# Pacing, an earlier root, interleaved transposes and sums from copies at the joint between two projections

## The chip, the cores and the metric

The kernel runs on one core of a Trainium2 chip. The metric is device time in microseconds (us): what one execution takes on the core. The engines are named PE (TensorE), DVE (VectorE), ACT (ScalarE), POOL (GpSimd) and SP (SyncE, which issues the transfers). Each works through its own instructions in the order in which the program gave them.

## The reference

Two transformer blocks on a sequence of 1024 tokens with 1024 channels, in float32. The part around the change is the end of the second block:

```python
merged = g_a * (o_a @ w_branch_a[l]) + g_b * (o_b @ w_branch_b[l])
x = x + merged @ w_out[l]
h2 = rms_norm(x, norm2[l])
x = x + jnp.square(jax.nn.relu(h2 @ w_up[l])) @ w_down[l]
return rms_norm(x, final_norm)
```

`rms_norm` multiplies a row by the reciprocal root of its mean square and by a gain per channel.

## The kernel before

**Precision.** Each float32 operand is split into a high part (a rounding copy on ACT, `e.hi`) and a low part (the difference, `e.lo`, on POOL or DVE). A product is three matmuls: high by high, low by high, high by low.

**Seven products.** The projection `merged @ w_out`, the up projection and the down projection are each cut in 2 x 2 quadrants and computed with seven products in place of eight (Strassen's scheme in Winograd's form). Products 2 to 7 need sums or differences of quadrants as operands: `cb`, `wr` (of weights, line 838), `ms` (of activations, `m_sums`), `s1` to `s4` (of the up projection's activations, `prep1`). The order of products is ORDER = (1, 6, 7, 4, 2, 5, 3); the text counts products of the output projection by their place in it, from 1 to 7. Each has four tiles of 12 matmuls of 512 columns (four `q` by three matmuls, for each of four row tiles).

**How order is made.** The program is written out by a Python generator that keeps a planned clock `e.t`, moved on by `e.pe` with each matmul. `e.at(dt, fn, tag)` puts a piece of work of another engine on a heap; it is written out when the planned clock reaches its time, or earlier by `e.need(tag)`. Nothing on the chip looks at this clock: it sets only the order on each engine. Instructions wait for the data by semaphores.

**Feeds.** A `Feed` (`FO` for the output projection, `F` for the up projection) holds a list of steps: a weight difference on DVE (`comb`) or a split (`split`: ACT, and with the next step the low part on POOL, or on DVE in 5 of 14 for `FO`). `ahead(n)` and `s.need(mark, n)` set a goal; up to it `tick` writes one step out each `gap` ns of planned time; a step that is not out when its operand is used is forced. `look` says how many steps further the loads are issued. `FO` has 72 steps: products 1 to 7 end at steps 8, 28, 36, 48, 56, 64, 72. In `F`, for the first three column groups (N0 = 3), steps 1 to 3 split operand 1; then for each q come the split of operand 2 and four differences (4 to 18); then three splits each for operands 4, 5, 6, 7 and 3.

**Stages around the change.** `merge` makes `mT` in eight rounds j and starts `FO`. `out2` runs the seven products; `out2_gather` adds each bank to the residual `x` (DVE, line 1554), takes a square sum (ACT, `sumsq`, tile `junk`) and, once both column halves are there, `f3` has POOL form the reciprocal root (`ry`, lines 117 and 118) and DVE scale the row (`xs`, line 1567). There are six row buffers, so rows 6 and 7 (`held`) are scaled when `prep0` has let go of the first four. `prep0` transposes the scaled rows of the first half into two banks in turn (`tp`); ACT copies each twice (`hh`, `hr`, lines 1677 and 1678) and DVE forms `hl` (line 1679). `prep1` does the second half: per k it transposes two banks, `p21` and `p22`, and DVE forms three sums straight from them with the first half's `r11` (line 1700), and the low part. `up_first` runs the up projection's products for three column groups: 3 tiles each for operands 1, 2, 4, 5, 6, 7, 3. At the end of the stage a helper joins generators: `prep0` is written between the matmuls of `out2`, its rest behind them; `prep1` between those of `up_first`, one step per four groups of three matmuls.

The helper records every matmul at line 99, every transpose at 104, and splits at 109 (high) and 112 (low), so rows are told apart by tile names.

Of the kernel before, what the change touches and what calls it, by code (L numbers as in the profile page):

```python
# [11 lines left out]
F32 = mybir.dt.float32  # L12
# [286 lines left out]
def block_kernel(ctx: ExitStack, tc: tile.TileContext, a: dict):  # L299
# [655 lines left out]
            e.mm(ps[:, c2], wl[:, c], h[:, c2], False, k == KT - 1)  # L955
            yield 327.0

    def interleave(main, side, start, every):

        side, n = side(), 0  # L960
        for _ in main:
            t = start()
            if side is not None and t is not None and e.t >= t:
                n += 1
                if n % every == 0:
                    try:
                        next(side)
                    except StopIteration:
                        side = None
        if side is not None:  # L970
            run(side)

    qsc = [[2.0 ** (2 * p + j - 2) for j in range(2)] for p in range(4)]
# [513 lines left out]
    def merge():  # L1487
        g_load(0)
        for j in range(8):
            if j < 7:  # L1490
                g_load(j + 1)
            parts = W.get(f"ab{j}", 1)
            if j == 5:
                for q in range(4):
                    FO.raw[q, "a", 1] = mT[q, 1]
                FO.load(0, 8)
            if j > 5:
                FO.ahead(8 * (j - 5))
            for half in range(2):
                ps2 = []  # L1500
                for b in range(2):
                    ps = e.mmt()
                    wh, wl = parts[b]
                    for k in range(4):
                        c = slice(k * 128, k * 128 + 128)
                        e.need(("o", 4 * b + k, half))
                        h, l = oT[4 * b + k, half]
                        e.mm(ps, wh[:, c], h, k == 0, False)
                        e.mm(ps, wh[:, c], l, False, False)
                        e.mm(ps, wl[:, c], h, False, k == 3)  # L1510
                        yield 650.0
                    g = gt.pop((b, j, half))
                    e.at(50, lambda ps=ps, g=g: V.scalar_tensor_tensor(out=g, in0=g, scalar=1.0, in1=ps,
                                                                       op0=ALU.add, op1=ALU.mult))
                    ps2.append(g)
                ga, gb = ps2
                e.at(800, lambda ga=ga, gb=gb: V.tensor_tensor(out=ga, in0=ga, in1=gb, op=ALU.add))
                mT[j, half] = ga
            if j >= 4:
                e.at(1800, lambda q=j - 4: m_sums(q), ("ms", j - 4))  # L1520
            W.pop(f"ab{j}")
# [10 lines left out]
    def out2():  # L1532
        for n, i in enumerate(ORDER):
            if n < 4:
                for t in range(4):
                    x2_load(i, t)
            if n >= 4:
                F.load(0, n - 3)
                F.ahead(6 * (n - 4))
            e.wide = i not in (5, 3)  # L1540
            yield from row_prod(FO, i, range(4), 16, out2_gather)

    def x2_load(i, t):
        t, ch = where(i, t)
# [6 lines left out]
    def out2_gather(i, t, ps):  # L1551
        t, ch = where(i, t)
        xt = x2[t, ch]
        V.scalar_tensor_tensor(out=xt, in0=ps, scalar=0.5, in1=xt, op0=ALU.mult, op1=ALU.add)
        if i not in (4, 2, 5, 3):
            return
        if ch == 0:
            ss2[t] = e.stat(name="ss2")
        ss = ss2[t]
        e.at(750, lambda: sumsq(xt, ss[:, ch:ch + 1]))  # L1560
        if ch == 1:
            def f3():
                POOL.tensor_tensor(out=ss[:, 2:3], in0=ss[:, 0:1], in1=ss[:, 1:2], op=ALU.add)
                r = e.rstd(ss[:, 2:3])
                xs = e.row("xs")
                for j in range(2):
                    V.tensor_scalar(out=xs[:, 512 * j:512 * j + 512], in0=x2[t, j], scalar1=r, scalar2=None, op0=ALU.mult)
                xs2[t] = xs

                def f4():  # L1570
                    for j in range(2):
                        SY.dma_start(out=x2_d[t * 128:(t + 1) * 128, 512 * j:512 * j + 512], in_=x2.pop((t, j)))
                e.at(2500, f4)
            if t < 6 or rows_free:
                e.at(1650, f3, ("xs2", t))
            else:
                held.append((f3, ("xs2", t)))
            xs2_t[t] = e.t + 4450


    F = Feed()
# [106 lines left out]
    def prep1():  # L1688
        for t in range(4, 8):
            e.need(("xs2", t))  # L1690
        for k in range(4):
            if k > 1:
                e.need(("s2", k - 2))
            two = e.ssp.tile([128, 1024], F32, name="S", tag="S") if k % 2 else None
            p21, p22 = (tr4(1, k + 4 * j, None if two is None else two[:, 512 * j:512 * j + 512]) for j in range(2))
            g1, g2 = gains[:, 2, k:k + 1], gains[:, 2, k + 4:k + 5]
            r11, r12 = HR.pop(("11", k)), HR.pop(("12", k))
            x21, s1, s3, s2 = (e.u(name="hr") for _ in range(4))
            h, l = HA["22", k] = e.u(F32R, "hh"), e.u(F32R, "hl")
            stt = lambda out, ps, g, y, op: V.scalar_tensor_tensor(out=out, in0=ps, scalar=g, in1=y, op0=ALU.mult, op1=op)  # L1700
            e.at(50, lambda p22=p22, h=h, g2=g2: ACT.activation(h, p22, AF.Copy, scale=g2))
            e.at(50, lambda p21=p21, x21=x21, g1=g1: ACT.activation(x21, p21, AF.Copy, scale=g1))
            e.at(800, lambda p21=p21, s3=s3, g1=g1, r11=r11: stt(s3, p21, g1, r11, SUB))
            e.at(1500, lambda p22=p22, s1=s1, g2=g2, x21=x21: stt(s1, p22, g2, x21, ADD))
            e.at(2200, lambda p22=p22, l=l, g2=g2, h=h: stt(l, p22, g2, h.bitcast(F32), SUB), ("A", "22", k))
            e.at(2900, lambda p22=p22, s2=s2, g2=g2, s3=s3: stt(s2, p22, g2, s3, ADD), ("s2", k))
            asplit("s1", k, s1, 2400, POOL)
            asplit("s3", k, s3, 4500, POOL)
            asplit("s2", k, s2, 5500, V)
            e.at(12000 + 1000 * k, lambda r12=r12, s2=s2: V.tensor_tensor(out=r12, in0=r12, in1=s2, op=SUB))  # L1710
            asplit("s4", k, r12, 14000 + 1000 * k, POOL)
            yield 872.0
        for t in range(4, 8):
            xs2.pop(t)

    def prod(ps, q, i, first=True, ahead=11):
        wh, wl = F.take((q, i), ahead)
        for k in range(4):
            e.need(("A", ANAME[i], k))
            h, l = HA[ANAME[i], k]  # L1720
            c = slice(k * 128, k * 128 + 128)
# [44 lines left out]
    def up_first():  # L1766
# [8 lines left out]
        for q in qs:  # L1775
            X[q] = ps = e.mmt()
            yield from prod(ps, q, 1, True, 6)
            e.at(50, lambda q=q, ps=ps: keep(1, q, ps), ("keep", q))
        for q in qs:
            ps = X.pop(q)  # L1780
            e.need(("keep", q))
# [74 lines left out]
                e.at(50, lambda q=q: keep(3, q, X[q]), ("u3", q))  # L1856
                e.at(750, lambda q=q: total(q, Vb[q], 3, "22"), ("c22", q))

    interleave(out2(), prep0, lambda: xs2_t.get(3), 2)
    interleave(up_first(), prep1, lambda: xs2_t[7], 4)  # L1860
    e.wide = True
    F.look = 11
    run(up_pairs(N0))
# [116 lines left out]
```

## Time and profile before

| | us |
|---|---|
| median of 3 runs | 1864.5 |
| lowest, highest | 1864.38, 1864.9 |
| the profiled execution | 1863.2 |
| its span, first to last instruction | 1861.5 |

The mean granted clock of TensorE over the span is 0.989 of full speed. All rows are of the one profiled execution; times in them count from its first instruction. "x12" is a count; a name such as `mm<-hh,fh` is the tile written, then the tiles read. A bracket behind a row is the idle time of the engine just before it, with what ended it.

### The profile page before, as it was taken

What the parts mean: (1) busy time and instruction counts of PE and PEld (TensorE: products, weight loads), DVE (VectorE), ACT (ScalarE), POOL (GpSimd) and SP (SyncE); (2) the same over time, 40 slices, a digit from 0 to 9 for tenths busy, and PEclk for the clock granted to TensorE, in tenths of its full rate; (3) what the DMA queues carried; (4) which work ended last, traced back from release to release, by engine and by line L of the source; (5) the groups of instructions that cost most, each with busy time, mean ns of one, the idle gap of its engine ahead of it and who ended that gap; (6) DMA issues with size and microseconds to landing.
All of it is one profiled execution on the core that took longest, in us unless ns stands there. A gap on an engine that the chain in (4) does not pass through costs nothing.

```text
span 1861.5 us, 25745 instructions
## 1 busy us (share of the span) xinstructions
PE 1802.8 (97%) x8957; PEld 1513.3 (81%) x8957; DVE 1132.7 (61%) x2081; ACT 962.3 (52%) x1979; POOL 733.7 (39%) x704
## 2 busy tenths in 40 slices
PE   7999999999999999999999999779999998999998
PEld 6888878898898898889888887558888876888886
DVE  6578783645454556655675485576443347766785
ACT  6455453447656667554565214465555554352444
POOL 4123242512212212212111425556544445775873
PEclk9999999999999999999999999889999999999999
DMA  7101132314222212120213923203635368444522
GB/s 203 34 24 35 35 114 69 125 35 92 80 46 85 76 39 60 57 71 26 63 38 107 300 68 119 75 11 128 218 127 183 126 240 303 158 151 138 170 85 91
DMA packets 189187, 195.69 MB, mean 105 GB/s; under 512 B 16944, under 2 KB 124160, under 8 KB 189056
## 3 DMA queue, kind: packets, MB, share of 16 engines
q1 hardware_dynamic: 189056, 194.04, 33.1%
q8 instruction: 70, 1.15, 0.3%
q14 instruction: 61, 0.50, 0.1%
HBM read 141.52 MB, written 54.04 MB: 105 GB/s over the span
## 4 chain that ended last, share of the span: by engine, by line
PE 86%; DVE 6%; issue 3%; ACT 3%; POOL 2%; DMA 1%; POOLq 0%; SPq 0%; ACTq 0%; DVEq 0%
PE mm L99 37%; PE mmmm L99 14%; PE mmT L99 9%; PE mmO L99 7%; PE mmo L99 5%; PE tp L104 4%; PE S L99 4%; PE O L99 4%; POOL fl L112 1%; DVE wr L838 1%; DVE s L1055 1%; ACT junk L404 1%; POOL ry L118 0%; DMA ha<-hid_d 0%; DVE sb L665 0%
## 5 line engine op out<-in xcount | busy, mean ns | idle before, releaser
L112 POOL TENSOR_TENSOR wl<-wr,wh 128x512 fp32r<-128x512 f32 x148 | 198.5, 1347 | 561.7 <-ACT wh L109 320.5
L99 PE MATMUL mm<-hh,wh 128*128 128x512 f32 (+1 forms) x792 | 313.8, 396 | 0.0
L99 PE MATMUL mm<-hl,wh 128*128 128x512 f32 (+1 forms) x792 | 310.1, 392 | 1.1 <-DVE hl L940 1.1
L99 PE MATMUL mm<-hh,wl 128*128 128x512 f32 (+1 forms) x792 | 309.5, 391 | 0.0
L112 POOL TENSOR_TENSOR fl<-wr,fh 128x512 fp32r<-128x512 f32 x161 | 228.7, 1434 | 146.4 <-ACT fh L109 122.1
L109 ACT CAST fh<-wr 128x512 fp32r<-128x512 f32 x216 | 130.4, 617 | 222.0 <-DVE wr L838 170.1
L656 ACT ACTIVATE sb<-sb,nm 128x128 f32<-128x128 f32 (+2 forms) x192 | 125.7, 655 | 149.4 <-DVE nm L650 99.0
L99 PEld LDWEIGHTS mm<-hh,wl 128*128 128x128 f32 x792 | 149.8, 189 | 32.5
L99 PEld LDWEIGHTS mm<-hl,wh 128*128 128x128 f32 x792 | 150.2, 190 | 26.1 <-DVE hl L940 1.6
L99 PEld LDWEIGHTS mm<-hh,wh 128*128 128x128 f32 x792 | 150.2, 190 | 25.3
L112 DVE TENSOR_TENSOR ptl<-tp,pth 128x512 fp32r<-128x512 f32 (+2 forms) x176 | 113.5, 646 | 79.8 <-ACT pth L109 75.8
L112 POOL TENSOR_TENSOR fl<-ha,fh 128x512 fp32r<-128x512 f32 x80 | 122.0, 1542 | 48.9 <-ACT fh L109 35.8
L109 ACT CAST pth<-tp 128x512 fp32r<-128x512 f32 (+2 forms) x176 | 96.4, 548 | 74.0 <-PE tp L104 69.8
L665 DVE TENSOR_SCALAR sb<-sb,rc 128x128 f32<-128x128 f32 (+2 forms) x192 | 97.6, 508 | 6.7
L104 PE MATMUL tp<-ident,sb 128*128 128x128 f32 x648 | 99.7, 272 | 1.3 <-DVE ptl L112 1.0
L109 ACT CAST wh<-wr 128x512 fp32r<-128x512 f32 x148 | 89.9, 617 | 20.7 <-DMA wr<-in_w_branch_a 16.1
L104 PEld LDWEIGHTS tp<-ident,sb 128*128 128x128 f32 x648 | 80.5, 140 | 22.9 <-DVE ptl L112 1.8
L838 DVE TENSOR_TENSOR wr<-wr 128x512 f32<-128x512 f32 x108 | 95.0, 880 | 1.6
L99 PE MATMUL O<-pth,v 128*128 128x256 f32 (+3 forms) x264 | 93.2, 361 | 0.0
L99 PE MATMUL mmmm<-fh 128*128 128x512 f32 x212 | 83.4, 393 | 6.7 <-ACT fh L109 6.7
L99 PE MATMUL mmmm<-fl,fh 128*128 128x512 f32 x212 | 83.8, 395 | 2.4 <-POOL fl L112 1.8
L99 PE MATMUL mmmm<-fh,fl 128*128 128x512 f32 x212 | 83.0, 391 | 0.0
(319 smaller groups left out, 4586.0 us busy)
## 6 DMA issues: line engine op xcount, KB each, us to landing
wr<-in_w_in SPq DMA_DIRECT2D x116, 256.0 KB, 3.4
ha<-hid_d SPq DMA_DIRECT2D x112, 256.0 KB, 3.7
wr<-in_w_up SPq DMA_DIRECT2D x64, 256.0 KB, 3.8
hid_d<-hc SPq DMA_DIRECT2D x64, 256.0 KB, 2.7
wr<-in_w_down SPq DMA_DIRECT2D x64, 256.0 KB, 4.2
hid_d<-pk SPq DMA_DIRECT2D x45, 256.0 KB, 3.8
wr<-in_w_out SPq DMA_DIRECT2D x32, 256.0 KB, 5.0
x_d<-x SPq DMA_DIRECT2D x32, 256.0 KB, 2.1
```

The costliest lines, as they stand in the source:

```text
L99: self.nc.tensor.matmul(out=out, lhsT=lhsT, rhs=rhs, start=start, stop=stop, skip_group_check=skip)
L104: self.nc.tensor.transpose(out, in_, ident)
L109: self.nc.scalar.copy(out, in_)
L112: (eng or self.nc.vector).tensor_tensor(out=out, in0=in0, in1=hi.bitcast(F32), op=ALU.subtract)
L404: ACT.activation(j[:, 0:n], src, AF.Square, accum_out=acc)
L656: ACT.activation(d[:, 0:w], d[:, 0:w], AF.Exp, bias=nm, scale=-1.0, accum_out=g.sm[:, j:j + 1])
L665: V.tensor_scalar(out=d[:, 0:w], in0=d[:, 0:w], scalar1=g.rc[:, j:j + 1], scalar2=None, op0=ALU.mult)
L838: eng.tensor_tensor(out=self.raw[dst], in0=self.raw[x], in1=self.raw[y], op=op)
L1055: V.tensor_tensor(out=nxt[:, a0:1040], in0=cur[:, a0:1040], in1=cur[:, a0 - n:1040 - n], op=ALU.add)
```

## The change

1. `FO` writes a step each 800 ns of planned time (1500 before); its goals are 8, then 20 steps in the last rounds of `merge` (8, 16 before), and in `out2` 20 ahead in the first two products and 28 after (16 before). `F` gets a goal of 8 in product 7 (before: 0, 6 and 12 in products 5 to 7).
2. In `out2_gather` the root is written 1650 ns after the gather as before, and the scaling in a function of its own at 3000 ns.
3. What is left of `prep0` after `out2` is returned by `interleave(..., True)` and written inside `up_first`, one step per two groups; `prep1` follows it in the same generator, one step per four groups.
4. In `prep1` both banks are copied out (`x21` on ACT as before, `x22` on DVE); the low part and the sums are formed from the copies, and the sums are queued behind the fourth transposes (`sums_a`). Transposes no longer wait for `s2`.

```diff
@@
     FO = Feed()
-    FO.look = 8
+    FO.look, FO.s.gap = 8, 800.0
@@
             if j > 5:
-                FO.ahead(8 * (j - 5))
+                FO.ahead(8 if j == 6 else 20)
@@
             if n >= 4:
                 F.load(0, n - 3)
-                F.ahead(6 * (n - 4))
+            if n == 6:
+                F.ahead(8)
             e.wide = i not in (5, 3)
-            yield from row_prod(FO, i, range(4), 16, out2_gather)
+            yield from row_prod(FO, i, range(4), 20 if n < 2 else 28, out2_gather)
@@
             def f3():
-                POOL.tensor_tensor(out=ss[:, 2:3], in0=ss[:, 0:1], in1=ss[:, 1:2], op=ALU.add)
-                r = e.rstd(ss[:, 2:3])
                 xs = e.row("xs")
                 for j in range(2):
-                    V.tensor_scalar(out=xs[:, 512 * j:512 * j + 512], in0=x2[t, j], scalar1=r, scalar2=None, op0=ALU.mult)
+                    V.tensor_scalar(out=xs[:, 512 * j:512 * j + 512], in0=x2[t, j], scalar1=rs[0], scalar2=None, op0=ALU.mult)
                 xs2[t] = xs
...
+            def f2():
+                POOL.tensor_tensor(out=ss[:, 2:3], in0=ss[:, 0:1], in1=ss[:, 1:2], op=ALU.add)
+                rs.append(e.rstd(ss[:, 2:3]))
+            e.at(1650, f2, ("rs2", t))
+
+            def f23():
+                e.need(("rs2", t))
+                f3()
             if t < 6 or rows_free:
-                e.at(1650, f3, ("xs2", t))
+                e.at(3000, f23, ("xs2", t))
             else:
-                held.append((f3, ("xs2", t)))
-            xs2_t[t] = e.t + 4450
+                held.append((f23, ("xs2", t)))
+            xs2_t[t] = e.t + 4900
@@ prep1
         for k in range(4):
-            if k > 1:
-                e.need(("s2", k - 2))
...
-            x21, s1, s3, s2 = (e.u(name="hr") for _ in range(4))
+            x21, x22 = raw[k] = e.u(name="hr"), e.u(name="hr")
...
-            e.at(800, lambda p21=p21, s3=s3, g1=g1, r11=r11: stt(s3, p21, g1, r11, SUB))
-            e.at(1500, lambda p22=p22, s1=s1, g2=g2, x21=x21: stt(s1, p22, g2, x21, ADD))
-            e.at(2200, lambda p22=p22, l=l, g2=g2, h=h: stt(l, p22, g2, h.bitcast(F32), SUB), ("A", "22", k))
-            e.at(2900, lambda p22=p22, s2=s2, g2=g2, s3=s3: stt(s2, p22, g2, s3, ADD), ("s2", k))
-            asplit("s1", k, s1, 2400, POOL)
-            asplit("s3", k, s3, 4500, POOL)
-            asplit("s2", k, s2, 5500, V)
-            e.at(12000 + 1000 * k, lambda r12=r12, s2=s2: V.tensor_tensor(out=r12, in0=r12, in1=s2, op=SUB))
-            asplit("s4", k, r12, 14000 + 1000 * k, POOL)
+            e.at(50, lambda p22=p22, x22=x22, g2=g2: V.tensor_scalar(out=x22, in0=p22, scalar1=g2, scalar2=None, op0=ALU.mult))
+            e.at(800, lambda x22=x22, l=l, h=h: e.lo(l, x22, h), ("A", "22", k))
+            if k == 3:
+                for n in range(4):
+                    e.at(1600 + 1500 * n, lambda n=n: sums_a(n, *raw.pop(n)), ("sa", n))
             yield 872.0
@@
+    def sums_a(k, x21, x22):
+        r11, r12 = HR.pop(("11", k)), HR.pop(("12", k))
+        s3, s2 = e.u(name="hr"), e.u(name="hr")
+        V.tensor_tensor(out=s3, in0=x21, in1=r11, op=SUB)
+        V.tensor_tensor(out=x21, in0=x21, in1=x22, op=ADD)
+        V.tensor_tensor(out=s2, in0=x22, in1=s3, op=ADD)
+        asplit("s1", k, x21, 700, POOL)
+        asplit("s3", k, s3, 4500, POOL)
+        asplit("s2", k, s2, 5500, V)
+        e.at(9000 + 1000 * k, lambda: V.tensor_tensor(out=r12, in0=r12, in1=s2, op=SUB))
+        asplit("s4", k, r12, 11000 + 1000 * k, POOL)
@@
-    interleave(out2(), prep0, lambda: xs2_t.get(3), 2)
-    interleave(up_first(), prep1, lambda: xs2_t[7], 4)
+    first = interleave(out2(), prep0, lambda: xs2_t.get(3), 2, True)
+
+    def preps():
+        if first is not None:
+            yield from first
+        for _ in range(200):
+            if e.t >= xs2_t[7]:
+                break
+            yield
+        for _ in prep1():
+            yield
+            yield
+    while first is not None and ("11", 3) not in HA:
+        next(first)
+    interleave(up_first(), preps, None, 2)
```

`prod` gets one more line, which writes a pending `sums_a` out before an operand that needs it.

## Rows read from the trace of the kernel before

**Rows 1.** Page, part 1: busy time of the engines.
```profile
PE 1802.8 (97%) x8957; PEld 1513.3 (81%) x8957; DVE 1132.7 (61%) x2081; ACT 962.3 (52%) x1979; POOL 733.7 (39%) x704
```

**Rows 2.** Windows by product: us, busy PE, PEld, DVE, ACT, POOL, clock, DMA, GB/s
```profile
1107.50:1118.40 10.90, 10.90 (x49) 9.03 (x49) 10.80 (x16) 1.14 (x2) 1.87 (x2) 1.00 0.29 95
1118.40:1136.10 17.70, 14.62 (x50) 10.79 (x50) 10.36 (x12) 6.44 (x12) 10.47 (x8) 0.81 0.30 103
...
1147.00:1159.10 12.10, 11.38 (x49) 8.84 (x48) 6.45 (x8) 7.40 (x16) 8.76 (x7) 1.00 0.51 146
...
1170.00:1181.20 11.20, 11.16 (x49) 8.91 (x48) 4.58 (x5) 6.55 (x15) 11.03 (x11) 1.00 0.12 47
1181.20:1210.00 28.80, 17.57 (x64) 12.16 (x64) 19.93 (x29) 9.33 (x22) 10.45 (x23) 0.76 0.28 103
1210.00:1219.60 9.60, 3.54 (x18) 2.31 (x17) 3.67 (x6) 5.50 (x10) 1.49 (x4) 0.79 0.13 49
1219.60:1230.80 11.20, 11.20 (x53) 9.33 (x52) 4.88 (x9) 4.70 (x8) 0.00 (x0) 0.88 0.00 0
1230.80:1246.40 15.60, 12.13 (x55) 9.62 (x54) 14.71 (x20) 12.90 (x24) 11.87 (x9) 0.89 0.00 1
1246.40:1255.00 8.60, 6.58 (x28) 4.94 (x28) 8.50 (x7) 7.08 (x13) 8.60 (x6) 1.00 0.00 0
```

**Rows 3.** Waits, 1172 to 1200: total us, times, longest.
```profile
DVE xs L1567 <- POOL ry L118: 9.2, 4, 4.8
...
PE mmo L99 <- DVE fl L112: 6.4, 3, 3.6
```

**Rows 4.** Timeline of POOL and DVE before the first scaled row.
```profile
1173.84 3.81 POOL L112 TENSOR_TENSOR fl<-wr,fh 128x512 fp32r<-128x512 f32 x3
...
1178.75 2.94 DVE L1567 TENSOR_SCALAR xs<-x,ry 128x512 f32<-128x512 f32 x2 [4.83 <-POOL ry L118]
```

**Rows 5.** Waits, 1200 to 1224.
```profile
PE tp L104 <- DVE hl L1679: 9.5, 5, 3.4
...
ACT junk L404 <- DVE x L1554: 6.5, 2, 4.4
```

**Rows 6.** Timeline of product 2: the last weight difference, and PE.
```profile
1122.00 0.69 DVE L838 TENSOR_TENSOR wr<-wr 128x512 f32<-128x512 f32 x1
...
1123.45 0.80 PE L99 MATMUL mmmm<-fh 128*128 128x512 f32 x1 [2.46 <-ACT fh L109]
```

**Rows 7.** Groups by shape, 1223 to 1258: count, busy us, mean ns, idle before.
```profile
L1710 DVE TENSOR_TENSOR hr<-hr 128x512 f32<-128x512 f32 x4 | 5.7, 1436 | 0.0
...
L112 DVE TENSOR_TENSOR hl<-hr,hh 128x512 fp32r<-128x512 f32 x4 | 5.1, 1286 | 0.0
L1700 DVE SCALAR_TENSOR_TENSOR hr<-S,gains,hr 128x512 f32<-128x512 f32 x6 | 4.4, 741 | 0.9 <-ACT hr L1702 0.9
...
L112 POOL TENSOR_TENSOR hl<-hr,hh 128x512 fp32r<-128x512 f32 x9 | 13.9, 1554 | 19.2 <-ACT hh L109 19.2
L112 POOL TENSOR_TENSOR fl<-wr,fh 128x512 fp32r<-128x512 f32 x6 | 9.9, 1655 | 0.8 <-ACT fh L109 0.8
```

**Rows 8.** Waits, 1224 to 1258.
```profile
PE mmo L99 <- POOL fl L112: 3.5, 1, 3.5
...
PE mm L99 <- POOL fl L112: 2.0, 1, 2.0
```

**Rows 9.** Chain that ended last, three pieces: start, us, what.
```profile
1219.97 3.93 PE mmo L99 x12
...
1230.24 0.87 PE S L104 x8
...
1257.26 2.72 PE mmo L99 x12
```

**Rows 10.** The tile `tp`: ACT's copies out of its banks, ns min/median/max.
```profile
L1677 ACT ACTIVATE hh<-tp,gains x8: 668/687/688, 1204.2 to 1220.0; 128x512 fp32r<-128x512 f32 x8
```

**Rows 11.** Timeline of DVE: a row's two scalings.
```profile
1219.44 0.88 DVE L1567 TENSOR_SCALAR xs<-x,ry 128x512 f32<-128x512 f32 x2 [0.64 <-PE tp L104]
```

More of the change, by code (lines that the diff above doesn't have):

```diff
@@ L956, in g_Tq, with interleave @@
             yield 327.0
-    def interleave(main, side, start, every):
+    def interleave(main, side, start, every, rest=False):
         side, n = side(), 0
+        if start is None:
+            start = lambda: 0.0
         for _ in main:
@@ L970, in interleave @@
         if side is not None:
+            if rest:
+                return side
             run(side)
@@ L1573, in f3 @@
                 e.at(2500, f4)
+            rs = []
+            def f2():
[5 more added lines that the diff above has]
+                f3()
             if t < 6 or rows_free:
-                e.at(1650, f3, ("xs2", t))
+                e.at(3000, f23, ("xs2", t))
             else:
-                held.append((f3, ("xs2", t)))
-            xs2_t[t] = e.t + 4450
+                held.append((f23, ("xs2", t)))
+            xs2_t[t] = e.t + 4900
     F = Feed()
@@ L1690, in prep1 @@
             e.need(("xs2", t))
+        raw = {}
         for k in range(4):
-            if k > 1:
-                e.need(("s2", k - 2))
             two = e.ssp.tile([128, 1024], F32, name="S", tag="S") if k % 2 else None
@@ L1696, in prep1 @@
             g1, g2 = gains[:, 2, k:k + 1], gains[:, 2, k + 4:k + 5]
-            r11, r12 = HR.pop(("11", k)), HR.pop(("12", k))
-            x21, s1, s3, s2 = (e.u(name="hr") for _ in range(4))
+            x21, x22 = raw[k] = e.u(name="hr"), e.u(name="hr")
             h, l = HA["22", k] = e.u(F32R, "hh"), e.u(F32R, "hl")
-            stt = lambda out, ps, g, y, op: V.scalar_tensor_tensor(out=out, in0=ps, scalar=g, in1=y, op0=ALU.mult, op1=op)
             e.at(50, lambda p22=p22, h=h, g2=g2: ACT.activation(h, p22, AF.Copy, scale=g2))
             e.at(50, lambda p21=p21, x21=x21, g1=g1: ACT.activation(x21, p21, AF.Copy, scale=g1))
-            e.at(800, lambda p21=p21, s3=s3, g1=g1, r11=r11: stt(s3, p21, g1, r11, SUB))
-            e.at(1500, lambda p22=p22, s1=s1, g2=g2, x21=x21: stt(s1, p22, g2, x21, ADD))
-            e.at(2200, lambda p22=p22, l=l, g2=g2, h=h: stt(l, p22, g2, h.bitcast(F32), SUB), ("A", "22", k))
-            e.at(2900, lambda p22=p22, s2=s2, g2=g2, s3=s3: stt(s2, p22, g2, s3, ADD), ("s2", k))
-            asplit("s1", k, s1, 2400, POOL)
-            asplit("s3", k, s3, 4500, POOL)
-            asplit("s2", k, s2, 5500, V)
-            e.at(12000 + 1000 * k, lambda r12=r12, s2=s2: V.tensor_tensor(out=r12, in0=r12, in1=s2, op=SUB))
-            asplit("s4", k, r12, 14000 + 1000 * k, POOL)
+            e.at(50, lambda p22=p22, x22=x22, g2=g2: V.tensor_scalar(out=x22, in0=p22, scalar1=g2, scalar2=None, op0=ALU.mult))
[3 more added lines that the diff above has]
+                    e.at(1600 + 1500 * n, lambda n=n: sums_a(n, *raw.pop(n)), ("sa", n))
             yield 872.0
@@ L1718, in prod @@
         for k in range(4):
+            e.need(("sa", k) if (ANAME[i], k) not in HA else ())
             e.need(("A", ANAME[i], k))
@@ L1778, in up_first @@
             e.at(50, lambda q=q, ps=ps: keep(1, q, ps), ("keep", q))
+        assert ("12", 3) in HA
         for q in qs:
```

## The prediction

> **What bounds the kernel.** I read the page first: TensorE (PE) is busy for 97% of the span [rows 1], so only PE's remaining waits can be won. Windows cut at the products of the stage that the diff touches show where they lie [rows 2]. Unit prices for PE come from the chain of waits [rows 9]: twelve matmuls (one product tile) take 2.72 us undisturbed, eight transposes 0.87 us. A product of the second output projection (48 matmuls) should take 10.9 us; what its window has beyond that is loss:
>
> - Product 2 (1118.4 to 1136.1): 17.7, loss 6.8.
> - Products 4 and 6: 12.1 and 11.2, loss 1.5 together.
> - Product 7 (1181.2 to 1210.0) also holds 16 transposes, 1.7: 12.6 wanted, 28.8 taken, loss 16.2.
> - The tail of `prep0` (1210.0 to 1219.6): 16 transposes alone, 1.7 wanted, 9.6 taken, loss 7.9.
> - First three tiles of `up_first`, 8.2 plus 16 transposes 1.7: 9.9 wanted, 11.2 taken, loss 1.3.
> - Next three, the same 9.9 wanted, 15.6 taken, loss 5.7. Then 8.6 holds 28 matmuls (6.4): loss 2.2.
>
> Together 41.6 us. Part of each loss is the clock: PEclk is below 1.0 in the disturbed windows, and the twelve matmuls just behind the tail of `prep0`, where PE had mostly stood idle, took 3.93 instead of 2.72 [rows 2, 9]. A removed wait therefore takes back slow matmuls too.
>
> The waits name the causes. In product 7, PE waits for operand splits on VectorE (DVE), and DVE waits for the reciprocal root on GpSimd (POOL) [rows 3]. The timeline shows why: POOL runs three splits in a row before it reaches the root, and DVE, which works in order, stands 4.83 us in front of `xs` with PE's splits behind it [rows 4]. The same order carries on behind it: ScalarE (ACT) waits for DVE's gathers, so the copies that free the transpose banks are late, and the transposes wait 9.5 us for DVE's `hl` [rows 5]. In product 2 the last weight difference leaves DVE at 1122.6, and PE stands 2.46 us for its split [rows 6]; DVE had been busy for 10.8 of the 10.9 us before [rows 2]. In `up_first`, PE waits 3.5 and 2.0 us for POOL's `fl` [rows 8], behind the `hl` splits of the activation sums.
>
> **The change, part by part.**
>
> *Pacing of the output operands* (gap 800, 20 ahead in the merge, then 20 and 28). There are 72 steps. One product is some 10.4 us of planned time, 7 steps at the old gap, 13 at the new. From step 20 at the start of product 1 the goals give 28, 41, 54 and 67 steps at the ends of products 1 to 4; product 7's last operand is step 72, reached early in product 5. Before, goals of 16 past the current mark left product 7's splits in products 6 and 7. So POOL has nothing but roots and a few splits of the next weights in products 6 and 7, and the 12.7 us of product 7 that are not transpose waits (16.2 less 3.5 in front of the late transposes, the longest wait of [rows 5] with its restart) go: I take 12, bounds 9 and 12.7. The work is the same; it lies under products 1 to 5, where POOL is busy for 8.8 of 12.1 us at most [rows 2]. Products 4 and 6: I take 1 of 1.5.
>
> Product 2 gains less. Its last difference is held up by a DVE that is already full, and the pacing takes only about two operations (a gather and idle of one operation, 0.69 each [rows 6]) from ahead of it. The difference ends some 1.3 us earlier, and with fewer slow matmuls I take 2.5 of 6.8; bounds 0 (DVE gets more contention) and 6.
>
> *Root taken early* (`f2` at 1650, scaling at 3000). No instruction is added; DVE meets `xs` about 1.35 us of plan later, when POOL's root is done. It is one mechanism with the empty POOL queue and its gain is in the 12 above; without it DVE would still stand there for a square sum and a root. `xs2_t` moves by 450 ns; the transposes start at the same even step of product 7 as before, and four steps fit, as before.
>
> *Rest of `prep0` inside `up_first`.* The four late transposes steps now lie between matmuls, one per six, so a bank is needed again only after some 3.6 us, while its readers take two ACT passes of 0.69 [rows 10] and one on DVE of 0.74 [rows 7]. The losses 3.5 + 7.9 + 1.3 = 12.7 go, less about 1.7 because ACT is nearly full there (two passes a step, square sums, `keep`): I take 11, bounds 8.5 and 12.7.
>
> What is late next: rows 6 and 7 can be scaled only when `prep0` ends, and `prep1` now begins in that same call. Before, two tiles lay in between. DVE needs `hl` and four scalings (two in 0.88 [rows 11]) while PE has only six matmuls (1.36) for cover: from the end of the last transposes some 3.3 us against 1.36 plus two transposes, so a loss of 1.3; bounds 0.5 and 3.
>
> *The next weights' feed* is 8 steps ahead at the end of the projection, not 12. By the ticks (1.5 us apart) step 14, the third tile's second operand, and step 19 are forced where they are needed. Each then costs an ACT pass (0.69 [rows 10]) and a POOL split (1.27), near 2 us, less the half microsecond before the low part is read: 1.5 each, 3 together; bounds 0 and 4.
>
> *Sums from copies.* Before: per k four DVE operations from PSUM, 0.74 each, 16 in all [rows 7]. After: one copy from PSUM (0.74 by the same row) and four operations with two SBUF inputs. With POOL quiet these take 0.69 [rows 6], beside POOL's splits 1.29 to 1.44, and POOL's own go from 1.27 (three in 3.81, [rows 4]) to 1.55 and 1.66 [rows 7]. DVE's 16 x 0.74 = 11.8 us become 4 x (0.74 + 4 x 0.69) = 14 to 4 x (0.74 + 4 x 1.44) = 26 us. In exchange banks come free at once, and `s2` holds no transposes back. But all sums come after the fourth transposes, so POOL is nearly idle for some 17 us and then gets eight `hl` splits and six `fl` together. Queue them in order at 1.3 to 1.7: the second tile of operand 4 waits about 2.5 (its `fl` sits behind the first sum), the first tile of operand 5 about 2.3 for `fl` and 1.4 for the last sum, later ones 0.8 together: 7, bounds 2 and 12.
>
> The Trainium skill, "SBUF — State Buffer", section "SBUF: two separate sides", speaks against this edit: a DVE operation with two SBUF inputs and a GpSimd operation that reads SBUF shut each other out for a whole instruction; one that reads PSUM and a single SBUF tensor is not on its list. By that rule the trace's two kinds are no accident (0.74 steady from PSUM, up to 1.44 with two SBUF inputs), and the sum would be that of the second rival, 1851, where the mix of the rows gives 1842.
>
> The edge into `up_first` so costs 1.3 + 3 + 7, and 0.7 for slow matmuls behind the waits: 12, where it cost 5.7 + 2.2 = 7.9; bounds of the change: 4 gained, 9 lost, I take 4.1 lost.
>
> **The sum.** 12 + 1 + 2.5 + 11 - 4.1 = 22.4. The profiled execution took 1863.2 (span 1861.5); 1840.8 after. The median of the runs is 1864.5, 1.3 above it: 1842. All bounds at once would be 12.7 + 1.5 + 6 + 12.7 + 4 = 37 (1827.5) and 9 + 0 + 0 + 8.5 - 9 = 8.5 (1856).
>
> **Rivals.**
>
> 1. *Look-ahead is blocked.* The steps are issued earlier, but DVE, full in product 1, and tiles not yet free hold them, and product 7 still waits. For it: the 10.8 of 10.9 us. Against: DVE is busy 6.45 of 12.1 us in product 4 [rows 2]. Only the transposes gain: 11 - 4.1 = 7, 1857.5. Chance 7%.
> 2. *The shared port decides.* All 16 two-input operations pay 1.44 and POOL 1.66, on PE's path: 16 x 0.75 = 12 us, 9 of them beyond what I put in. Gain 13, 1851. For it: [rows 7]. Against: POOL and DVE also wait for each other's results, and then run alone. Chance 14%.
> 3. *POOL becomes the bound behind the sums: slower.* Each of the 15 tiles of operands 4, 5, 6, 7 and 3 waits for its `fl`. Without the 7 us that I put in for POOL the gain is 29.4; slower by 3.7 needs waits of 33.1, so it decides from 2.2 us a tile on. At 2.5 it costs 37.5 and gives 1864.5 + 8.1 = 1872.6. For it: waits of 3.5 and 2.0 already stand in [rows 8], and the sums now start late. Against: 12 sums and 21 weights at 1.66 are 55 us of POOL, and PE has 21 tiles and 48 transposes, 62 us. Chance 4%.
> 4. *The new waits hide*: DVE and POOL run ahead of PE, the 12 us of the edge fall to 1, the gain is 33: 1831. For it: POOL had 19 idle us there [rows 7] only because its inputs were late. Against: PE is in order and the first wait moves all that follows. Chance 6%.
>
> **How the numbers follow.** Forecast 66% (own range 1833 to 1850), rivals as above, no measurable change 3%. Faster by over 0.2% (3.7 us, about what a measurement can tell from none) is 66 + 7 + 14 + 6 = 93%, same 3%, slower 4%. The range 1831 to 1855 leaves out most of rival 1, rival 3, no change, half of rival 4 and the edges of the others: about 2 in 10.
>
> **What would show it.** Right: product 7 within 14 us, no wait of DVE `xs` for POOL `ry` above 1 us, no idle of PE in front of transposes in product 7, transposes between matmuls of `up_first`; the worst waits left are in product 2 (DVE) and in operands 4 and 5 of `up_first` (POOL `fl`), `sums_a` operations above 1 us. Wrong: splits of output operands still in product 7 (rival 1), POOL full and PE waiting in every later tile (rival 3), or new waits ahead of product 1, in the merge, which I count at nothing because DVE's gates there have four banks of 2.72 us as cover.

## The result and the profile after

The changed kernel took 1852.6 us (median; 1850.2 to 1853.8) against 1864.7 of the kernel before beside it: ratio 0.9934 [0.9917, 0.9951], 12.05 us faster. The profiled execution took 1852.6 with a span of 1850.9, where the one before had 1861.5. That lies inside the range, but it is little more than half of the 22.5 that I forecast, and close to the 1851 of the second rival.

The page first: PE is at 97% as before, and DVE and POOL have 16.0 and 9.7 us more busy time than in [rows 1], although no POOL operation was added (704 as before) and only four on DVE.

```profile
PE 1798.5 (97%) x8957; PEld 1510.1 (82%) x8957; DVE 1148.7 (62%) x2085; ACT 962.7 (52%) x1979; POOL 743.4 (40%) x704
```

Windows by product, columns as in [rows 2]. In order: product 2, 4, 6, 7, the first six tiles of `up_first`, its other fifteen tiles.

```profile
1118.50:1132.40 13.90, 11.72 (x51) 9.07 (x50) 12.20 (x16) 6.59 (x13) 10.57 (x8) 1.00 0.31 100
1143.20:1154.10 10.90, 10.90 (x49) 9.03 (x49) 6.49 (x8) 6.70 (x16) 10.90 (x8) 1.00 0.36 105
1165.00:1175.90 10.90, 10.90 (x50) 9.01 (x49) 4.35 (x8) 3.41 (x9) 2.64 (x9) 1.00 0.60 192
1175.90:1189.80 13.90, 13.15 (x66) 10.42 (x65) 11.57 (x17) 8.02 (x18) 9.84 (x17) 1.00 0.49 183
1189.80:1218.10 28.30, 24.69 (x121) 19.32 (x119) 16.18 (x24) 17.28 (x31) 3.95 (x6) 0.94 0.04 14
1218.10:1277.60 59.50, 45.81 (x180) 34.54 (x180) 51.25 (x46) 30.35 (x55) 48.20 (x31) 0.93 0.15 45
```

The same two windows of `up_first` in the kernel before, which the prediction had cut only as far as its eighth tile: the six tiles with the tail of `prep0` took 36.4 (the sum of three rows of [rows 2]), and the other fifteen this long:

```profile
1246.40:1289.90 43.50, 41.48 (x182) 33.57 (x181) 27.82 (x29) 24.47 (x44) 34.27 (x24) 1.00 0.19 56
```

With the same unit prices as in the prediction (a tile 2.72, eight transposes 0.87), the loss in each stretch and what became of it, in us:

| stretch | wanted | loss before | loss after | gained | forecast |
|---|---|---|---|---|---|
| product 2 | 10.9 | 6.8 | 3.0 | 3.8 | 2.5 |
| products 4 and 6 | 21.8 | 1.5 | 0 | 1.5 | 1 |
| product 7 with 16 transposes | 12.6 | 16.2 | 1.3 | 14.9 | 15.5 (12, and 3.5 of the transposes' 11) |
| six tiles, 48 transposes | 21.5 | 14.9 | 6.8 | 8.1 | |
| fifteen tiles | 40.8 | 2.7 | 18.7 | -16.0 | |
| the last two together | 62.3 | 17.6 | 25.5 | -7.9 | 3.4 (7.5 of the transposes, -4.1 at the edge) |
| sum | | 42.1 | 29.8 | 12.3 | 22.4 |

The spans differ by 10.6, so 1.7 lies outside these windows. What lies ahead of the fifteen tiles came about within 0.6 of the forecast or better; then 16 us are given back in the fifteen tiles, where the granted clock was 0.93 against 1.00 before.

The waits of product 7 and its surroundings (1165 to 1205) hold no operand split and no `xs` that waits for POOL's `ry`, which [rows 3] had with 6.4 and 9.2 us. The square-sum chain still waits, but no scaling waits for its root; the transposes wait 1.9 us for scaled rows:

```profile
POOL ss L1580 <- ACT junk L404: 15.0, 7, 5.8
...
PE tp L104 <- DVE xs L1570: 1.9, 2, 1.4
```

PE's waits in the fifteen tiles, from its timeline (start, us, what, and in the bracket the idle time with what ended it):

```profile
1219.50 0.50 PE L99 MATMUL mm<-hh,fl 128*128 128x512 f32 x1 [0.63 <-POOL fl L112]
...
1227.38 0.80 PE L99 MATMUL mmo<-hh,fl 128*128 128x512 f32 x1 [4.86 <-POOL fl L112]
...
1238.74 0.50 PE L99 MATMUL mmo<-hl,fh 128*128 128x512 f32 x1 [1.27 <-POOL hl L112]
...
1240.44 0.50 PE L99 MATMUL mm<-hh,fl 128*128 128x512 f32 x1 [0.50 <-POOL fl L112]
1243.84 0.50 PE L99 MATMUL mmo<-hh,fl 128*128 128x512 f32 x1 [0.38 <-POOL fl L112]
1247.23 0.50 PE L99 MATMUL mm<-hh,fl 128*128 128x512 f32 x1 [0.37 <-POOL fl L112]
1250.62 0.50 PE L99 MATMUL mmo<-hh,fl 128*128 128x512 f32 x1 [0.38 <-POOL fl L112]
...
1270.39 0.47 PE L99 MATMUL mm<-hh,fh 128*128 128x512 f32 x1 [0.89 <-ACT fh L109]
...
1277.63 0.77 PE L99 MATMUL mmmm<-hh,fh 128*128 128x512 f32 x1 [4.26 <-DVE pk L1783]
```

Read four things. One wait of 4.86 stands at the second tile of operand 4. From 1240.44 to 1250.62 the waits come at a step of 3.39 us, while a tile takes 2.72: PE goes at the pace of POOL. And 4.26 us stand at the very end, for a bank that an addition on DVE frees. The nine waits add up to 13.5 of the 18.7 us; the other 5.2 are restarts and the slow matmuls behind the waits.

What DVE and POOL did meanwhile, from their timelines:

```profile
1221.91 0.69 DVE L1725 TENSOR_TENSOR hr<-hr 128x512 f32<-128x512 f32 x1
...
1224.05 1.60 POOL L112 TENSOR_TENSOR hl<-hr,hh 128x512 fp32r<-128x512 f32 x1 [4.61 <-ACT hh L109]
1224.56 1.64 DVE L1726 TENSOR_TENSOR hr<-hr 128x512 f32<-128x512 f32 x1
1225.61 3.40 POOL L112 TENSOR_TENSOR fl<-wr,fh 128x512 fp32r<-128x512 f32 x2
...
1233.57 1.74 POOL L112 TENSOR_TENSOR fl<-wr,fh 128x512 fp32r<-128x512 f32 x1
...
1243.75 1.73 POOL L112 TENSOR_TENSOR hl<-hr,hh 128x512 fp32r<-128x512 f32 x1
1244.25 5.17 DVE L1731 TENSOR_TENSOR hr<-hr 128x512 f32<-128x512 f32 x3
1245.44 1.74 POOL L112 TENSOR_TENSOR fl<-wr,fh 128x512 fp32r<-128x512 f32 x1
...
1250.53 1.29 POOL L112 TENSOR_TENSOR hl<-hr,hh 128x512 fp32r<-128x512 f32 x1
...
1267.87 1.77 DVE L838 TENSOR_TENSOR wr<-wr 128x512 f32<-128x512 f32 x1 [1.18 <-POOL fl L112]
```

The twelve sums of `sums_a` as groups (line 1725 is `s3`, 1726 `s1`, 1727 `s2`), 1222 to 1252:

```profile
L1726 DVE TENSOR_TENSOR hr<-hr 128x512 f32<-128x512 f32 x4 | 5.7, 1412 | 0.1
L1727 DVE TENSOR_TENSOR hr<-hr 128x512 f32<-128x512 f32 x4 | 4.9, 1223 | 0.0
L1725 DVE TENSOR_TENSOR hr<-hr 128x512 f32<-128x512 f32 x4 | 3.8, 954 | 0.0
```

As long as POOL waits, a sum on DVE takes 0.69. From 1224 on, where both have work, each operation of either takes 1.6 to 1.8. So the three means above are no prices: six of the twelve sums took 1.64 to 1.77 and six 0.68 or 0.69. From 1233.57 to 1250.53 POOL works without a gap, ten operations in 16.96 us, one each 1.70; DVE's three differences (line 1731) take 5.17 there, 1.7 each. From 1250.53, with no sum left, POOL is at 1.29 again. PE's pace follows from this: from 1238.65 POOL alternates one `fl` of a tile with one `hl` of a sum. Two operations at 1.70 are 3.40 a tile; two at 1.29 would be 2.58, less than the tile's 2.72. The low part `fl` of the second tile is written out behind the first sum's `hl`, and that `hl` stands 4.61 for ACT's `hh`: so PE gets its 4.86. At the end, the next weights' differences (line 838) on DVE wait for POOL's splits, the additions of the last tiles stand behind them in DVE's order, and PE stands 4.26 for the bank.

### The profile page after: what moved, and what is told of

Read it like the earlier page. It is cut to its first block, busy times and chain, and to the rows that moved or that the text cites. A ratio compares the mean times of both kernels' runs of the same rounds, so it can differ in the third digit from the quotient of the medians.

```text
span 1850.9 us, 25759 instructions
## 1 busy us (share of the span) xinstructions
PE 1798.5 (97%) x8957; PEld 1510.1 (82%) x8957; DVE 1148.7 (62%) x2085; ACT 962.7 (52%) x1979; POOL 743.4 (40%) x704
## 4 chain that ended last, share of the span: by engine, by line
PE 87%; DVE 5%; issue 3%; ACT 2%; POOL 2%; DMA 1%; POOLq 0%; SPq 0%; ACTq 0%; DVEq 0%
PE mm L99 38%; PE mmmm L99 15%; PE mmT L99 10%; PE mmO L99 7%; PE mmo L99 5%; PE tp L104 4%; PE S L99 4%; PE O L99 4%; POOL fl L112 1%; DVE s L1059 1%; DVE wr L838 0%; DMA ha<-hid_d 0%; ACT junk L404 0%; POOL ry L118 0%; DVE sb L665 0%
## 5 line engine op out<-in xcount | busy, mean ns | idle before, releaser
L109 ACT CAST wh<-wr 128x512 fp32r<-128x512 f32 x148 | 89.9, 617 | 27.9 <-DMA wr<-in_w_branch_a 15.8
L99 PE MATMUL mmmm<-hh,fh 128*128 128x512 f32 x208 | 82.0, 394 | 4.3 <-DVE pk L1783 4.3
```

Of the source, the lines that this page charges most:

```text
L99: self.nc.tensor.matmul(out=out, lhsT=lhsT, rhs=rhs, start=start, stop=stop, skip_group_check=skip)
L109: self.nc.scalar.copy(out, in_)
```

## The experiments

All are compared with the kernel before on the same chip, and a gain is against that kernel's median (1863.2 to 1864.0). "The whole change" is the 12.05 above. Differences of under some 3 us between two experiments are not separated by their intervals.

### The parts, one after the other

**Part 1 alone** on the kernel before:

```diff
-    FO.look = 8
+    FO.look, FO.s.gap = 8, 800.0
...
-                FO.ahead(8 * (j - 5))
+                FO.ahead(8 if j == 6 else 20)
...
-                F.ahead(6 * (n - 4))
+            if n == 6:
+                F.ahead(8)
...
-            yield from row_prod(FO, i, range(4), 16, out2_gather)
+            yield from row_prod(FO, i, range(4), 20 if n < 2 else 28, out2_gather)
```

> The kernel before with part 1 alone (steps of the output operands each 800 ns, goals 20 and 28, F's goal 8). Theory A (the look-ahead is the gain; parts 3 and 4 lose on balance because the bunched sums meet POOL): product 7 loses its waits for splits (12.7 us), product 2 some 4, products 4 and 6 1.5; the tail of prep0 stays near 8 us of loss, and the two feed steps forced in up_first cost about 3: some 15 us faster than before, about 1849, so faster than the whole change (1852.6). Theory B (the root is needed for it: DVE still stands in front of xs until POOL's root is there, and PE's operands and banks wait behind it): at most half of that, 1856 or more. Theory C (parts 3 and 4 pay): slower than the whole change by 5 us or more, 1858.

Measured 1854.0, ratio 0.9948 [0.9934, 0.9961], 10.0 faster, between the 1849 of one theory and the 1856 of the other. Its waits from 1165 to 1210:

```profile
PE tp L104 <- DVE hl L1680: 11.9, 4, 6.6
...
DVE xs L1568 <- POOL ry L118: 11.6, 6, 2.0
```

The operand splits are gone from product 7 and the longest wait for the root fell from 4.8 to 2.0. But all six scalings still wait, and PE now pays for it at the transposes. The look-ahead is not blocked, so the first rival falls.

**Parts 1 and 2** (the root in `f2` at 1650, the scaling at 3000):

```diff
+            def f2():
+                POOL.tensor_tensor(out=ss[:, 2:3], in0=ss[:, 0:1], in1=ss[:, 1:2], op=ALU.add)
+                rs.append(e.rstd(ss[:, 2:3]))
+            e.at(1650, f2, ("rs2", t))
...
-                e.at(1650, f3, ("xs2", t))
+                e.at(3000, f23, ("xs2", t))
...
```

> Parts 1 and 2: pacing, and the root written ahead of the scaling. Theory A: within 2 us of part 1 alone (about 1848), since an empty POOL queue makes the root prompt without it; the waits of DVE xs for POOL ry fall below 1 us each. Theory B: 5 us or more faster than part 1 alone.

Measured 1846.8, 0.9909 [0.9895, 0.9922], 17.2 faster and 7.2 better than part 1 alone. The wait of `xs` for `ry` has left the list; what is left of 1165 to 1210:

```profile
PE tp L104 <- DVE hl L1688: 6.9, 5, 2.1
```

So the root has a price of its own with POOL's queue empty: six rows at some 2.0 us of waiting on DVE (11.6 in all). That the two were one mechanism was wrong.

**Parts 1 to 3**, the sums still straight from the banks:

```diff
-    interleave(out2(), prep0, lambda: xs2_t.get(3), 2)
-    interleave(up_first(), prep1, lambda: xs2_t[7], 4)
+    first = interleave(out2(), prep0, lambda: xs2_t.get(3), 2, True)
...
+    interleave(up_first(), preps, None, 2)
```

> The whole change without part 4: pacing, root and interleaved transposes, with the second half's sums formed straight from the banks as before (DVE operations from PSUM at 0.74 us, each k's sums behind its own transposes). Theory A (copies and bunching cost): the 5 us wait of the second tile of operand 4 and the 4.3 us wait for a bank at the end of up_first shrink, 6 to 10 us faster than the whole change, 1843 to 1847. Rival D (banks held until the sums are formed keep the transposes back, which is what part 4 is for): PE waits in front of the transposes of k 2 and 3, same as the whole change or slower, 1852 to 1858.

Measured 1840.8, 0.9878 [0.9865, 0.9891], 23.2 faster. Part 3 is worth 6.0 over parts 1 and 2, and part 4 costs 11.1 (23.2 less 12.05). Windows of product 2, product 7, and the 21 tiles of `up_first`:

```profile
1118.20:1132.10 13.90, 11.74 (x51) 9.09 (x50) 12.22 (x16) 6.59 (x13) 10.57 (x8) 1.00 0.33 101
1175.60:1189.50 13.90, 13.15 (x66) 10.43 (x65) 11.56 (x18) 8.05 (x18) 9.83 (x17) 1.00 0.49 185
1189.50:1267.60 78.10, 68.46 (x301) 53.86 (x300) 53.29 (x65) 47.31 (x85) 47.61 (x37) 0.96 0.13 38
```

The first two are as long as those of the whole change. The third is 78.1, a loss of 15.8 over 62.3, against 28.3 + 59.5 = 87.8 and 25.5: 9.7 of the 10.8 by which the two spans differ lie here. DVE is busy for 53.3 us in it, and for 67.4 in the same stretch of the whole change (16.2 + 51.3). Its groups by shape, 1205 to 1262:

```profile
L1723 DVE TENSOR_TENSOR hr<-hr 128x512 f32<-128x512 f32 x4 | 5.7, 1444 | 0.0
...
L1713 DVE SCALAR_TENSOR_TENSOR hr<-S,gains,hr 128x512 f32<-128x512 f32 x6 | 4.4, 741 | 1.9 <-ACT hr L1715 1.9
```

Sums from a bank and one SBUF tensor take 0.74 beside the same POOL splits; the one sum with two SBUF inputs (line 1723) takes 1.44 on the mean. The only wait in front of PE's transposes after 1195 is the one that the whole change also has, for scaled rows:

```profile
PE tp L104 <- DVE xs L1570: 1.9, 2, 1.4
```

So with the sums straight from the banks no transpose waited for a bank, and the early release for which part 4 was made had nothing to win here.

**Part 4 alone** on the kernel before:

```diff
-            e.at(800, lambda p21=p21, s3=s3, g1=g1, r11=r11: stt(s3, p21, g1, r11, SUB))
...
+            e.at(50, lambda p22=p22, x22=x22, g2=g2: V.tensor_scalar(out=x22, in0=p22, scalar1=g2, scalar2=None, op0=ALU.mult))
+            e.at(800, lambda x22=x22, l=l, h=h: e.lo(l, x22, h), ("A", "22", k))
+            if k == 3:
+                for n in range(4):
+                    e.at(1600 + 1500 * n, lambda n=n: sums_a(n, *raw.pop(n)), ("sa", n))
...
```

> The kernel before with part 4 alone: copies out of the banks, sums bunched behind the fourth transposes; pacing, root and the place of the transposes as before. Theory (part 4 costs by itself, because POOL's sum splits start late and stand in front of weight splits): slower than before by 3 to 12 us, 1867 to 1876. Rival (part 4 pays where prep1 stands far ahead of its use, and costs only in the new place): within 2 us of before or faster.

Measured 1875.9, 1.007 [1.0058, 1.0083]: 12.7 slower. PE's waits, 1195 to 1320:

```profile
...
PE mmmm L99 <- DVE pk L1770: 4.6, 1, 4.6
...
```

The 4.6 for the bank at the end is there again, without any of the other parts. The cost of part 4 is its own.

### Why part 4 costs

Two causes were open: that DVE and POOL stretch each other's operations, or that the sums come all at once, in a poor order.

**The low parts of three sums on DVE** instead of POOL, all else as in the whole change:

```diff
-        asplit("s1", k, x21, 700, POOL)
-        asplit("s3", k, s3, 4500, POOL)
+        asplit("s1", k, x21, 700, V)
+        asplit("s3", k, s3, 4500, V)
...
-        asplit("s4", k, r12, 11000 + 1000 * k, POOL)
+        asplit("s4", k, r12, 11000 + 1000 * k, V)
```

> The whole change with the low parts of s1, s3 and s4 (12 operations) moved from POOL to DVE; the bunched sums and copies stay. Theory Q (PE's weight splits stand in POOL's order behind sum splits whose inputs are not ready, and the backlog carries on to the end of up_first): the waits of PE for POOL fl and hl after 1220 us shrink from about 9 us to under 3, the 4.3 us wait for a bank at the end goes too, 8 to 14 us faster than the whole change: 1839 to 1845. Theory L (DVE and POOL shut each other out, so the pairs of 1.7 us are the bound): also faster, but through shorter operations: the three sums of each k take 0.69 to 0.9 us on average in place of 1.2. Rival R (DVE has no room for 12 more): PE waits for DVE hl instead, 1850 or slower.

Measured 1844.5, 0.9895 [0.9882, 0.9909], 19.1 faster: 7.0 better than the whole change, though DVE has twelve operations more. All 2097 of them are busy for as long as the 2085 of the whole change, by the page:

```profile
PE 1796.1 (98%) x8957; PEld 1508.1 (82%) x8957; DVE 1148.7 (62%) x2097; ACT 962.5 (52%) x1979; POOL 726.0 (39%) x692
```

The timelines of DVE and POOL, and DVE's groups by shape, 1205 to 1262:

```profile
1224.13 1.27 POOL L112 TENSOR_TENSOR fl<-wr,fh 128x512 fp32r<-128x512 f32 x1 [4.53 <-ACT fh L109]
1224.17 1.77 DVE L1725 TENSOR_TENSOR hr<-hr 128x512 f32<-128x512 f32 x1
1225.98 0.69 DVE L1726 TENSOR_TENSOR hr<-hr 128x512 f32<-128x512 f32 x1
...
1227.92 1.28 POOL L112 TENSOR_TENSOR fl<-wr,fh 128x512 fp32r<-128x512 f32 x1 [2.52 <-ACT fh L109]
```

```profile
L1725 DVE TENSOR_TENSOR hr<-hr 128x512 f32<-128x512 f32 x4 | 4.9, 1230 | 0.0
...
L1726 DVE TENSOR_TENSOR hr<-hr 128x512 f32<-128x512 f32 x4 | 2.8, 692 | 0.1
L1727 DVE TENSOR_TENSOR hr<-hr 128x512 f32<-128x512 f32 x4 | 2.7, 684 | 0.0
```

The eight sums of lines 1726 and 1727 had means of 1412 and 1223 ns in the whole change; the four of line 1725 rose from 954 to 1230. The twelve together fell from 14.4 to 10.4 us. The wait for the bank at the end is 0.7 instead of 4.3. This edit takes twelve operations off POOL and also shortens DVE's, so by itself it does not tell POOL's load from the stretching.

**Each k's sums right behind its own transposes**, not all behind the fourth:

```diff
-            if k == 3:
-                for n in range(4):
-                    e.at(1600 + 1500 * n, lambda n=n: sums_a(n, *raw.pop(n)), ("sa", n))
+            e.at(1600, lambda n=k: sums_a(n, *raw.pop(n)), ("sa", k))
```

> The whole change, but each k's sums are queued 1600 ns behind its own transposes instead of all four behind the fourth. Copies from the banks stay. Theory A1 (bunching is the cost): POOL starts its splits of sums about 10 us earlier, the second tile of operand 4 waits under 2.5 us in place of 4.9, and the end of up_first no longer waits 4.3 us for a bank: 6 to 10 us faster, 1843 to 1847. Theory A2 (the stretch of operations with two SBUF inputs beside POOL is the cost, whenever they run): within 3 us of the whole change, because the same pairs of 1.7 us operations only move.

Measured 1849.0, 0.9921 [0.9908, 0.9935], 14.9 faster: 2.9 better than the whole change, with intervals that overlap. A single wait of 7.5 for POOL's `fl` stands in its list, and the one for the bank at the end is gone. Of the 11.1 that part 4 costs, bunching is at most a small part.

**The low parts of `s1` 2800 ns later**, so that the `fl` of operand 4's second tile goes ahead of them on POOL:

```diff
-        asplit("s1", k, x21, 700, POOL)
+        asplit("s1", k, x21, 3500, POOL)
```

> The whole change with the splits of s1 written 3500 ns behind each sum instead of 700; same instructions, same engines, only POOL's and ACT's order moves, so that the weight splits of operand 4 come ahead of the sum splits. Theory Q (order: PE's weight split stands behind a sum split whose input is not ready): the 4.9 us wait and its slow matmuls go, the 4.3 us wait for a bank at the end of up_first stays, 3 to 7 us faster than 1852.6: 1846 to 1850. Theory L (the stretch of DVE and POOL beside each other is the bound, whatever their order): within 2 us of 1852.6, as the same pairs are only waited for later.

Measured 1850.9, 0.9937 [0.9925, 0.995], 12.3 faster: the same as the whole change. PE's waits, 1195 to 1320:

```profile
PE mmo L99 <- POOL hl L112: 4.3, 3, 1.7
PE mmo L99 <- ACT hh L109: 4.1, 3, 1.7
PE mmmm L99 <- DVE pk L1783: 2.6, 1, 2.6
```

A group of DVE's sums and one of POOL's splits, 1205 to 1262:

```profile
L1727 DVE TENSOR_TENSOR hr<-hr 128x512 f32<-128x512 f32 x4 | 7.1, 1766 | 0.0
...
L112 POOL TENSOR_TENSOR hl<-hr,hh 128x512 fp32r<-128x512 f32 x12 | 19.7, 1651 | 0.0
```

The wait of 4.86 is gone, and 8.4 us of waits for the parts of `s1` stand in its place. The sums of line 1727 take 1.77 and POOL's splits 1.65, as in the whole change or more. The order only decides who waits.

So what is shown is this: part 4 costs 11 to 13 us, operations of DVE and POOL on its copies stretch each other to 1.7, and no new order tried takes the cost away. How much of the 11.1 is the stretching and how much the sums that start late no run separates; with the low parts on DVE 4.1 of it stays.

**The old goals for the next weights** (0, 6 and 12 steps), all else as in the whole change:

```diff
-            if n == 6:
-                F.ahead(8)
+                F.ahead(6 * (n - 4))
```

> The whole change, but F's goals in the output projection as before (0, 6, 12 in products 5 to 7 in place of 8 in product 7). Theory: the third tile's second operand and the first of operand 4 are no longer forced where they are needed, which costs 3 us in the whole change (waits for ACT fh and POOL fl of 0.5 to 0.9 with their restart), and the next split comes 1 to 2 steps earlier, ahead of the first sum on POOL: 3 to 8 us faster, 1844 to 1850. Rival: the feed was not the cause, the same steps are forced one tile later; within 2 us of 1852.

Measured 1849.6, 0.9921 [0.9908, 0.9935], 14.0 faster, 2.0 better than the whole change, which the intervals don't separate. Its longest waits are still 4.1 for `fl` and 4.3 for the bank.

### Is there a better version

**Sums from the banks, with the three low parts on DVE** (parts 1 to 3 and the same edit of `asplit`):

> Without part 4 (sums straight from the banks, 1840.8) and with the low parts of s1, s3 and s4 on DVE. Theory Q: of the remaining losses after 1205 us some 5 are PE waiting for POOL fl; 3 to 5 us faster than 1840.8: 1836 to 1838. Rival R (DVE's order is now what holds PE up): 1841 or slower.

Measured 1839.2, 0.9865 [0.9852, 0.9879], 24.4 faster: 1.2 over parts 1 to 3, not separated. Where the sums already read a bank, there is little left to free; a new wait of 2.6 for DVE's `hl` stands in the list.

**Sums from the banks, with the old goals of the feed:**

> Without part 4 (1840.8) and with F's goals as before. Theory: the forced steps cost 2.4 + 0.8 + 1.2 + 1.1 us of waits for ACT fh and POOL fl there; 3 to 5 us faster, 1836 to 1838. Rival: the early splits fall into product 7, where ACT copies the transposes out, and give it back there; within 1.5 us of 1840.8.

Measured 1838.7, 0.9864 [0.9851, 0.9878], 24.9 faster: 1.7 over parts 1 to 3, not separated, and less than the 3 to 5 expected. PE's waits, 1195 to 1320:

```profile
PE mmo L99 <- POOL fl L112: 3.7, 3, 1.7
PE tp L104 <- DVE xs L1569: 1.9, 2, 1.4
```

**The same, with `prep1` one step later**, so that rows 6 and 7 have time to be scaled (one more `yield` ahead of `prep1`):

> Sums from the banks, feed as before (1838.7), and prep1's first step two groups of three matmuls later, so that PE has twelve matmuls in place of six between the last transposes of prep0 and the first of prep1 that need rows 6 and 7. Theory: the waits of the transposes for DVE xs (1.6 + 0.7 with their restart and slow matmuls, near 3 us) shrink below 1: 1836 to 1837.5. Rival: prep1's results are then late by 1.3 us at operand 4, and it comes back as waits for DVE hl: 1838 to 1840.

Measured 1838.1, 0.987 [0.9855, 0.9885], 25.1 faster, the same. The wait in front of the transposes fell to 0.5, and came back at POOL:

```profile
PE mmo L99 <- POOL fl L112: 6.2, 3, 3.4
...
PE tp L104 <- DVE xs L1569: 0.5, 1, 0.5
```

**The same, with the low parts of `s3` and `s4` on DVE:**

> As the run with prep1 one step later, and the low parts of s3 and s4 (8 operations) on DVE, s1's left on POOL. Theory Q: POOL has only weight splits and four of s1 to do, the waits for POOL fl at operand 5 (0.96 and 1.0) go: 1834 to 1836.5, the fastest kernel so far. Rival: DVE's order holds the adds of operand 6 and 7 up; 1838 or slower.

Measured 1838.9, 0.987 [0.9857, 0.9884], 24.3 faster, the same again; the wait is now 4.0 for a DVE `hl`, and 3.5 for `fl`.

These four versions, all without part 4, are some 12 to 13 us better than the whole change and 24 to 25 faster than the kernel before. Why all four stop near 1838 to 1839 stays open: each edit moved a wait and did not remove it. A version in which POOL has fewer of the weights' splits in this stretch was not tried.

## Why the prediction was right or wrong, step by step

**Pacing and root.** The place and the sum were right: product 7 took 13.9 us (forecast within 14), and gained 14.9 of the 15.5. The division was wrong. I put the root in as one mechanism with the empty queue and gave it nothing of its own; by the runs part 1 brings 10.0 and the root 7.2. An empty queue shortens the wait of `xs` from 4.8 to 2.0; it cannot remove it, because the square sum and three small POOL operations still lie between the gather and the scaling, and DVE stands in order. The 3.5 in front of the late transposes of product 7 came with these parts too, and not with part 3: with parts 1 and 2 alone product 7 took 13.95 us.

**Product 2** gained 3.8, not 2.5; it was 13.9 with part 1 alone too, so this belongs to the pacing. DVE is still busy for 12.2 of its 13.9 us.

**Products 4 and 6** lost nothing any more: 10.9 each.

**Transposes in `up_first`.** The six tiles with 48 transposes took 28.3 against 36.4, a gain of 8.1 that already holds the start of `prep1`. That start cost more than the 1.3 that I took: from 1198.55 to 1206.12 PE did eight transposes and twelve matmuls, 3.6 us of work, in 7.6, a loss of 4.0. The waits themselves are 1.41 and 0.46; slow matmuls behind them make up much of the rest. It was not won back by the one try at it: with `prep1` one step later (without part 4) the time stayed.

**Feed.** Forecast 3 for two forced steps. The four starts of PE around them, at 1212.65, 1214.21, 1218.14 and 1219.50, come 0.64, 0.99, 0.63 and 0.79 later than a matmul's 0.23 would have them: 3.05. But with the old goals only 2.0 and 1.7 came back in the two tries, neither separated from nothing.

**Sums from copies: the step that failed.** I put it in at 7, with 0.7 for slow matmuls, against the 7.9 that the edge had cost: +0.2 in all. It measured -11.1 on top of parts 1 to 3, and -12.7 alone. Without this step the sum is 22.2, and the kernel without it gained 23.2. So the sum of the other steps was right to 1 us, though not their division: parts 1 and 2 brought 17.2 where their terms made 12.5 (12 + 1 + 2.5 - 3), and part 3 brought 6.0 of its 9.7 (11 - 1.3). The miss of the total is the term of the sums. Four things in it were wrong:

- I gave the second tile of operand 4 2.5 us. It waited 4.86, because POOL stood 4.61 for the `hh` of the first sum ahead of that tile's `fl`.
- I let POOL run at 1.3 to 1.7. For 17 us behind 1233.57 it ran at 1.70 throughout, since DVE always had an operation with two SBUF inputs beside it.
- I put 0.8 on everything behind operand 5's first tile. PE was held at 3.39 a tile for the three steps from 1240.44 to 1250.62, 0.67 over each, and 4.26 us with slow matmuls behind them came at the end, through differences on DVE that waited for POOL and additions that stood behind them.
- I used means of groups as prices. The twelve sums show that such a mean can be a mix of 0.69 (POOL idle) and 1.64 to 1.77 (POOL at work). Their total was not what failed: the twelve (14.4) and the four low parts of `x22` (0.68 or 0.69 each) took 17.1 us on DVE, inside my 11.0 to 23.0 (16 x 0.69 to 16 x 1.44). The waits that they and POOL's slower splits caused were.

This is the second rival's mechanism, but not its sum. That rival let all sixteen operations pay 1.44 on PE's path; by the timeline six paid 1.64 to 1.77 and ten 0.68 or 0.69, and PE lost its time at POOL's `fl` and at the end. That 1852.6 came so near to the rival's 1851 is therefore in part luck. The Trainium skill, "SBUF — State Buffer", section "SBUF: two separate sides", which I quoted and weighed below the mix of the rows, agrees with the runs on which operations collide: those with two SBUF inputs took 1.7 beside POOL's splits, those from a bank and one SBUF tensor 0.74. On the length it does not agree: shut out for a whole instruction, a pair would take 1.98 (0.69 + 1.29), and 1.70 was measured. The mechanism deserved more weight than I gave it. Taking POOL's splits of the sums away brings 7.0 us back; changing only the order brings 0.2 in one run and 2.9 in another, neither separated from nothing.

**The other rivals.** Look-ahead was not blocked. The third, with POOL as the bound of every later tile, is there in small: 0.67 us a tile between 1240 and 1251, where 2.2 on fifteen tiles would have been needed. The fourth, all new waits hidden, falls with the 25.5 of loss.

## What to carry to other kernels

A copy out of a PSUM bank is meant to free the bank early, but it turns a later operation that reads the bank and one SBUF tensor into one with two SBUF inputs, which took 1.7 us here beside a busy POOL instead of 0.74. Look first whether anything waits for the bank, and count what POOL does in that stretch. A group's mean duration may be a mix of two prices; read the single operations in the timeline and ask which price the change moves them to. When an in-order engine waits for a short result of another engine, clearing the other's queue isn't enough: write the producer out one step ahead of the consumer as well.

## What was not expected of the hardware

- With both queues full, operations of DVE (0.69 alone) and of POOL (1.29 alone) started 1.70 us apart on both engines, for 17 us: neither the 1.29 of a full overlap nor the 1.98 of one strictly after the other.
- In the run with the low parts on DVE, POOL still had the weights' splits. There a DVE sum beside POOL's `fl` of 1224.13 took 1.77, and the next, with POOL idle until 1227.92, took 0.69: the longer time comes and goes from one instruction to the next.
